# Modulation steps, h^T and scores moved in a two-layer hybrid backbone on one core

## The chip, the core and the metric

The kernel runs on one core of a Trainium2 chip, as one launch. Its time is the device time in microseconds (us), here the median of the runs shown. The engines are TensorE (PE; its weight loads are listed as PEld), VectorE (DVE), ScalarE (ACT), GpSimd (POOL) and SyncE (SP, which only issues DMAs). Each runs its own stream of instructions in order, and they meet at semaphores.

## What is computed

Two layers over 512 latent tokens and, in the first layer and as keys and values in the second, 256 context tokens, all with 1024 channels in float32. Each layer is a sandwich: half a SwiGLU FFN, a token mixer, half a SwiGLU FFN. The mixer is a chunked gMLP in layer 0 and grouped-query attention (8 query heads, 2 key/value heads, RMS-normalised q and k, rotary positions) in layer 1. Cut to what matters here:

```python
m = silu(c) @ w_mod + b_mod                 # 9 vectors of 1024 for each layer and condition
h = x * (1 + scale) + shift                 # modulate
y = (silu(h @ w_g) * (h @ w_u)) @ w_out     # FFN, 1024 -> 2 x 2816 -> 1024
x = layer_norm(ALPHA * x + 0.5 * gate * y, ln_g, ln_b)
# attention: s = q k^T, p = softmax(s), o = p v, then @ w_o; the same kind of closing
```

There are two conditions, one for the latent and one for the context tokens; the last modulation vectors are needed for the latent tokens only.

## The kernel before

Every matrix product is made from float32 values split in two parts of a shorter type: ScalarE casts a high part (`hi`), VectorE subtracts it to make a low part (`lo`), and three matmuls (hi hi, hi lo, lo hi) add up in PSUM. A weight tile comes in by a DMA on SP (`raw`, ring of 6), is split into `w` (ring of 8, `W_BUFS`) and is used some tiles later. `pump(n)` makes up to n splits as far as the ring has room; `release(n)` says that n tiles are used up.

There are six sublayers: FFN, gMLP, FFN (layer 0), FFN, attention, FFN (layer 1). The first, third and fourth are FFNs over 768 tokens in a Strassen form (`tile_strassen`, kind "s"): 22 tiles f, each of seven products (T2, T3, T1, B21 and so on) of 12 matmuls with 384 columns; the first eight tiles (`OPENED`) have two of their products made ahead. Then `out_proj` runs over n = 22 (24 after the gMLP) activation tiles in two halves of the channels: a step x is one weight tile and 18 matmuls, for six blocks of 128 tokens. The last six tiles of the second half (`CLOSE`) are kept for the closing (`End.inner`): block by block the rest of the products, the gated sum (L753, L764), LayerNorm statistics (L765), `rs` (a power on POOL, L184), z normalised on ScalarE (L1911, L1901), then the transposes of the block before (h^T, `h_transposes`) and their modulation (L601, L599) and split (L615, L617). Blocks that are left over are made by `make_h`, called through `self.hooks` from the next sublayer's first projection.

The modulation vectors of later sublayers are made on VectorE as a filler. A step of `mod_unit` multiplies one 128 x 512 tile of w_mod (`mraw`, loaded by SP) into an accumulator, for each of one or two conditions (`light` means one). Eight steps make half a vector; the eighth ends in a `partition_all_reduce` on POOL for each condition and a small DMA on POOL that adds the row to DRAM (L383, L384). `fill` does one step, and counts down `pending` (read-backs of finished vectors); `fill_pair` does two steps if `light`. In the tiles from f = 8 on one `fill_pair` goes with product T3; in `out_proj` most steps x have one. `MOD_PLAN` says which vectors a sublayer makes: 48 steps in the first, 96 in the gMLP, 32 in the third and 64 in the fourth. What is left is done at the closing's beginning.

`out_proj` runs with VectorE and ScalarE pinned, that is in the order of the program; TensorE, SP and most of POOL always are. Elsewhere (attention, the closings) the framework's planner puts their instructions in order by its own costs.

In attention, `token_proj` multiplies blocks of 128 tokens with eight weight tiles. For the second half of q it has three groups of blocks (0 and 1; 2; 3), between which `between` is called. Scores of unit n (a head and a block) go to a pair of PSUM banks, of which there are two (`PAIRS`); VectorE takes the maximum (L1435), ScalarE the exponential (L1443), which frees the pair.

## Time and profile before

| | before |
|---|---|
| median of 3 runs | 2837.98 us (2836.8 to 2839.62) |
| profiled execution, its own time | 2836.91 us |
| its span, first to last instruction | 2835.1 us |
| TensorE busy | 2777.8 us, 98% |
| VectorE busy | 2101.0 us, 74% |
| ScalarE busy | 1164.2 us, 41% |
| POOL busy | 540.4 us, 19% |
| mean granted TensorE clock | 0.996 of full |

Busy times are unions over the span: matmuls overlap in the pipeline, so the mean length of one, times their number, is more than the busy time. [...] A wait is idle time of an engine with the instruction, on which engine, that ended it. The names in a row are those of the tiles: `ps` and `pp` PSUM banks and pairs of banks, `w` split weights, `acc` modulation accumulators, `z` the residual stream.

### The profile page before, as it was taken

The page shows a single profiled execution, that of the slowest core. Times are in us where ns is not written, and L with a number is a line of the kernel's source. Part 1 is how long each engine was busy: PE and PEld are TensorE (multiplying, and loading weights), DVE is VectorE, ACT ScalarE, POOL GpSimd, SP SyncE. Part 2 cuts the span into 40 slices and gives each one's busy share as a digit, 9 for nine tenths or more (in the row PEclk, how much of TensorE's full clock was granted, in tenths as well). Part 3 has the DMA queues.
Part 4 walks back from the last instruction along what each step waited for, and adds up shares of the span by engine and source line. Part 5 has one row for each costly group of instructions (what it writes and reads, how often), then busy time and mean ns, then how long its engine had stood idle before and what let it go on. Part 6 is the DMA issues. An engine that isn't in the chain of part 4 may idle for free.

```text
span 2835.1 us, 40732 instructions
## 1 busy us (share of the span) xinstructions
PE 2777.8 (98%) x14454; PEld 2503.0 (88%) x14454; DVE 2101.0 (74%) x3680; ACT 1164.2 (41%) x2244; POOL 540.4 (19%) x605
## 2 busy tenths in 40 slices
PE   7999999999999999999999999999999999999998
PEld 5999988788899988899999879999988788888886
DVE  6988888577687786698887659888886598634345
ACT  7433332532355532453334236333432666623322
POOL 1000143333321132200013220001233121000001
PEclk9999999999999999999999999999999999999999
DMA  7443376355565474344336534433585424354352
GB/s 230 136 131 117 107 236 212 113 195 189 187 181 161 148 252 136 122 142 136 120 112 209 172 111 133 143 121 119 153 296 175 141 67 88 117 156 130 116 167 86
DMA packets 398675, 429.99 MB, mean 152 GB/s; under 512 B 28488, under 2 KB 287624, under 8 KB 398472
## 3 DMA queue, kind: packets, MB, share of 16 engines
q1 hardware_dynamic: 364360, 319.40, 36.6%
q0 software_dynamic: 34112, 108.00, 12.2%
q8 instruction: 113, 1.85, 0.3%
q14 instruction: 90, 0.74, 0.1%
HBM read 366.10 MB, written 63.41 MB: 151 GB/s over the span
## 4 chain that ended last, share of the span: by engine, by line
PE 86%; DVE 5%; issue 3%; ACT 3%; DMA 2%; POOL 1%; SPq 0%; DVEq 0%; POOLq 0%; ACTq 0%
PE ps L89 85%; PE pp L89 1%; DMA raw<-in_w_mod_dram 1%; ACT z L1911 1%; DVE w L89 1%; POOL acc L383 1%; ACT q L601 1%; DVE comb L89 1%; DMA mraw<-in_w_mod_dram 1%; POOL rs L184 0%; DMA raw<-in_ffn_w_in_dram 0%; DVE w L156 0%; DVE z L89 0%; DVE acc L89 0%; DVE q L1340 0%
## 5 line engine op out<-in xcount | busy, mean ns | idle before, releaser
L89 PE MATMUL ps<-comb,w 128*128 128x384 f32 x5544 | 970.6, 335 | 6.2 <-ACT w L155 2.4
L89 PEld LDWEIGHTS ps<-comb,w 128*128 128x128 f32 x5544 | 961.1, 188 | 11.5 <-ACT w L155 3.0
L89 PE MATMUL ps<-w,acts 128*128 128x512 f32 x3768 | 861.3, 390 | 0.0
L89 PEld LDWEIGHTS ps<-w,acts 128*128 128x128 f32 x3768 | 707.3, 188 | 146.5
L89 ACT CAST w<-raw 128x512 fp32r<-128x512 f32 x630 | 388.3, 620 | 844.4 <-PE ps L89 741.1
L89 DVE TENSOR_TENSOR w<-raw,w 128x512 fp32r<-128x512 f32 x630 | 448.6, 719 | 243.9 <-ACT w L89 243.7
L89 PE MATMUL ps<-h,w 128*128 128x384 f32 (+2 forms) x2304 | 445.6, 353 | 0.2 <-DVE w L156 0.2
L89 PEld LDWEIGHTS ps<-h,w 128*128 128x128 f32 x2304 | 403.0, 188 | 37.7 <-DVE w L156 0.4
L89 DVE SCALAR_TENSOR_TENSOR acc<-mraw,cs,acc 128x512 f32<-128x512 f32 x378 | 278.5, 773 | 15.3 <-DMA mraw<-in_w_mod_dram 15.1
L89 PE MATMUL ps<-w,h 128*128 128x512 f32 x1200 | 276.7, 391 | 2.8 <-ACT h L615 2.8
L89 PEld LDWEIGHTS ps<-w,h 128*128 128x128 f32 x1200 | 225.0, 188 | 50.9 <-ACT h L615 3.6
L383 POOL PARTITION_ALL_REDUCE acc<-acc x56 | 203.4, 3635 | 283.9 <-DVE acc L89 262.3
L89 POOL DMA_DIRECT2D q<-act x226 | 128.7, 611 | 563.5 <-DVE acts L89 296.9
L89 DVE TENSOR_TENSOR q<-q,ps 128x384 f32<-128x384 f32 (+1 forms) x258 | 143.8, 557 | 123.2 <-PE ps L89 102.9
L89 POOL DMA_DIRECT2D act<-stage x84 | 48.3, 575 | 976.9 <-DVE stage L89 930.5
L89 ACT CAST w<-sums 128x512 fp32r<-128x512 f32 x198 | 122.7, 620 | 239.9 <-DVE sums L302 117.6
L89 DVE TENSOR_TENSOR acts<-q,acts 128x384 fp32r<-128x384 f32 (+1 forms) x262 | 150.4, 607 | 9.3 <-ACT acts L89 9.3
L89 ACT CAST acts<-q 128x384 fp32r<-128x384 f32 (+1 forms) x262 | 126.2, 519 | 55.2 <-DVE q L89 36.5
L89 DVE TENSOR_TENSOR w<-sums,w 128x512 fp32r<-128x512 f32 x198 | 135.6, 685 | 1.7 <-ACT w L89 1.7
L156 DVE TENSOR_TENSOR w<-raw,w 128x512 fp32r<-128x512 f32 x114 | 75.4, 687 | 26.6 <-ACT w L155 26.0
L184 POOL TENSOR_TENSOR rs<-ve,mhalf 128x1 f32<-128x1 f32 (+3 forms) x47 | 42.1, 896 | 260.2 <-DVE ve L181 133.9
L155 ACT CAST w<-raw 128x512 fp32r<-128x512 f32 x114 | 67.9, 626 | 55.1 <-PE ps L89 31.8
(206 smaller groups left out, 2173.7 us busy)
## 6 DMA issues: line engine op xcount, KB each, us to landing
raw<-in_ffn_w_in_dram SPq DMA_DIRECT2D x400, 256.0 KB, 3.0
mraw<-in_w_mod_dram SPq DMA_DIRECT2D x256, 256.0 KB, 3.5
raw<-in_ffn_w_out_dram SPq DMA_DIRECT2D x176, 256.0 KB, 3.1
q<-act POOLq DMA_DIRECT2D x216, 192.0 KB, 4.3
act<-stage POOLq DMA_DIRECT2D x74, 384.0 KB, 2.9
raw<-in_gmlp_w_in_dram SPq DMA_DIRECT2D x96, 256.0 KB, 4.3
zhat<-z POOLq DMA_DIRECT2D x26, 512.0 KB, 2.9
raw<-in_gmlp_w_out_dram SPq DMA_DIRECT2D x48, 256.0 KB, 3.0
```

The costliest lines, as they stand in the source:

```text
L89: return self.tc.keep_in_program_order(f(*args, **kwargs))
L155: self.act.copy(hi, src)
L156: self.lows.append((key, lambda: self.dve.tensor_tensor(lo, src, hi.bitcast(F32), ALU.subtract)))
L184: self.last_rstd = self.nc.gpsimd.tensor_tensor(rs, ve, self.mhalf[:, 0:1].to_broadcast([P, n]), ALU.pow).ins
L383: nc.gpsimd.partition_all_reduce(accs[c], accs[c], P, bass_isa.ReduceOp.add)
L601: self.act.activation(h32[:, kk], ps[:, s], AF.Identity, bias=bi, scale=sc)
L1911: k.act.activation(k.z[b], k.z[b], AF.Identity, bias=nb, scale=rs)
```

## The change

- `tile_strassen`: tiles f = 8, 12, 16 and 20 call `fill_pair` a second time, with product B21. In the first FFN's `out_proj` an extra `fill` comes with every eighth step x, not every fourth. The second `fill` of a pair no longer counts down `pending`.
- `token_proj`: where hooks are waiting (the first projections after the first and fourth FFN), a hook is also called between the two halves of the second group; before, hooks came only behind a group.
- Attention: behind the first group of q's second half stand only the transposes of q (`first_turned`); behind the second group come scores 0 and 1, the second key head's transposes and their softmax; score 2 with its softmax comes in the middle of the third group. Weights of the next product are pumped there at k = 0 to 3 only (`ahead`), the others from the loop over units on.
- Attention's closing: for the last block, `pump` is called behind the first half of the channels only; both halves still release.
- The last closing (`last`): for blocks 0 to 2 the product and sum with the LayerNorm's rows follow at once rather than behind the next block's sums. VectorE does the first 512 channels with two fused instructions and no help from ScalarE; ScalarE and POOL do the others. The last block's four instructions are reordered, so that the first half is done and sent before the second.

```diff
@@ -496,12 +496,12 @@
             mods.insert(0, self.vectors_rest())
         self.filler = (s for u in mods for s in u)
 
-    def fill(self, n=1):
+    def fill(self, n=1, count=1):
 
         for _ in range(n):
             with self.behind():
                 for x in self.pending:
-                    x[0] -= 1
+                    x[0] -= count
                 due = [x for x in self.pending if x[0] < 0]
                 self.pending = [x for x in self.pending if x[0] >= 0]
                 for _, f in due:
@@ -512,7 +512,7 @@
 
         self.fill()
         if self.light:
-            self.fill()
+            self.fill(1, 0)
 
     @contextmanager
     def behind(self):
@@ -770,7 +770,7 @@
         for half in range(2):
             self.products(banks[half], b, acts, ws[half * n : half * n + n])
             if after:
-                after()
+                after(half)
         return [lambda half=half: self.add_gated(b, half, banks[half], factor, st) for half in range(2)]
 
     def stats(self, nblocks):
@@ -822,7 +822,7 @@
                     self.fill(int(self.light))
                 elif half or x < n - 1:
                     self.fill_pair()
-                    if prev is None and x % 4 == 3:
+                    if prev is None and x % 8 == 3:
                         self.fill()
         assert not residual
         rest = [acts.of(f) for f in orders[1][n - CLOSE :]]
@@ -985,7 +985,7 @@
         step(b3, "T1", lambda: add(w, w, b3))
         if opened is None:
             g = temp()
-            step(b1, "B21", lambda: act.activation(g, b1, AF.Silu), True)
+            step(b1, "B21", lambda: act.activation(g, b1, AF.Silu), True, int(fills > 1))
         c = temp()
         for _ in self.combining or ():
             pass
@@ -1016,7 +1016,7 @@
         acts = Acts(self, FF, TOK, KEPT, READ_BACK, f"act{l}{i}_")
         for f in range(FF):
             opened = self.begun.pop(min(self.begun)) if self.begun else None
-            self.tile_strassen(lambda: acts.place(f), opened, int(f > 7))
+            self.tile_strassen(lambda: acts.place(f), opened, int(f >= OPENED) * (1 + int(f % 4 == 0)))
             if f == OPENED - 1:
                 self.filler_raw()
         self.out_proj(acts, l, i, 0.5, end, prev, 2 if prev else 12)
@@ -1098,7 +1098,7 @@
         self.out_proj_latent(acts, l, i, 0.5, end, prev)
 
 
-    def token_proj(self, blocks, evacuate, fills=1, between=None):
+    def token_proj(self, blocks, evacuate, fills=1, between=None, inside=None, ahead=KD):
 
         banks = {}
 
@@ -1130,13 +1130,18 @@
                             self.flush()
                         evacuate(b, banks[b])
                 self.flush()
+                if k == KD // 2 - 1 and group is groups[-1] and inside:
+                    inside()
+                if k == KD // 2 - 1 and group is groups[1 % len(groups)] and between is None:
+                    self.hook()
                 if group is groups[-1]:
                     self.release(1)
-                    if k < KD - 1:
+                    if k < min(ahead, KD - 1):
                         self.pump(2)
                     self.fill(fills + int(fills and k == 4))
             self.hook()
-        self.pump(2)
+        if ahead == KD:
+            self.pump(2)
 
     def gmlp(self, l, i, nblocks, end, prev):
         nc, io, dve, act = self.nc, self.io, self.dve, self.act
@@ -1485,15 +1490,12 @@
                 for h in range(4)
             ]
 
-        def first_scores():
+        def first_turned():
             for b in range(2):
                 q_transposed(0, b)
+
+        def first_scores():
             sc = [scores(n) for n in range(PAIRS)]
-            for n in range(PAIRS):
-                state[n] = softmax(*sc[n])
-
-        def next_scores():
-            sc = [scores(n) for n in range(PAIRS, AHEAD)]
             k_transposed(1)
             for x in sc:
                 state[x[0]] = softmax(*x)
@@ -1508,7 +1510,12 @@
         k_transposed(0)
         for b in range(2):
             q_norm(0, b)
-        q_proj(1, between=(first_scores, next_scores))
+
+        def next_scores():
+            for n in range(PAIRS, AHEAD):
+                state[n] = softmax(*scores(n))
+
+        q_proj(1, between=(first_turned, first_scores), inside=next_scores, ahead=KD // 2)
         for b in range(2, NB_LAT):
             q_norm(0, b)
         new_qT(0, 1)
@@ -1572,9 +1579,10 @@
             after = None
             if b == NB_LAT - 1:
 
-                def after():
+                def after(half):
                     self.release(4)
-                    self.pump()
+                    if not half:
+                        self.pump()
 
             return self.close(b, banks, outputs(1), wo, 1.0, st[b], after), st[b]
 
@@ -1920,8 +1928,15 @@
     def last(self, nblocks, close):
 
         k = self.k
-        late = None
         k.dve = Pinned(k.tc, k.nc.vector)
+        first, second = slice(0, 512), slice(512, D)
+
+        def scaled(b, mu, rs, s):
+            z = k.z[b][:, s]
+            k.dve.scalar_tensor_tensor(z, z, mu, self.g[:, s], ALU.subtract, ALU.mult)
+            k.dve.scalar_tensor_tensor(z, z, rs, self.b[:, s], ALU.mult, ALU.add)
+            k.sp.dma_start(k.io["out"][0, b * P : b * P + P, s], z)
+
         for b in range(nblocks):
             adds, st = close(b)
             for add in adds:
@@ -1929,25 +1944,17 @@
             mv = k.sm([2], "mv")
             k.dve.bn_aggr(mv, st)
             rs = k.rstd(mv[:, 1:2], 1, eps=Z_EPS)
-            if late:
-                late()
             if b == nblocks - 1:
-                z, mu = k.z[b], mv[:, 0:1]
-                for s in (slice(0, 512), slice(512, D)):
-                    k.dve.scalar_tensor_tensor(z[:, s], z[:, s], mu, self.g[:, s], ALU.subtract, ALU.mult)
-                for s in (slice(0, 512), slice(512, D)):
-                    k.dve.scalar_tensor_tensor(z[:, s], z[:, s], rs, self.b[:, s], ALU.mult, ALU.add)
-                    k.sp.dma_start(k.io["out"][0, b * P : b * P + P, s], z[:, s])
+                scaled(b, mv[:, 0:1], rs, first)
+                scaled(b, mv[:, 0:1], rs, second)
                 break
             nb = k.norm_bias(mv, rs)
-
-            def late(b=b, rs=rs, nb=nb):
-                for eng, s in ((k.dve, slice(0, 512)), (k.nc.gpsimd, slice(512, D))):
-                    z = k.z[b][:, s]
-                    k.act.activation(z, z, AF.Identity, bias=nb, scale=rs)
-                    eng.tensor_tensor(z, z, self.g[:, s], ALU.mult)
-                    eng.tensor_tensor(z, z, self.b[:, s], ALU.add)
-                    k.sp.dma_start(k.io["out"][0, b * P : b * P + P, s], z)
+            z = k.z[b][:, second]
+            k.act.activation(z, z, AF.Identity, bias=nb, scale=rs)
+            k.pool.tensor_tensor(z, z, self.g[:, second], ALU.mult)
+            k.pool.tensor_tensor(z, z, self.b[:, second], ALU.add)
+            scaled(b, mv[:, 0:1], rs, first)
+            k.sp.dma_start(k.io["out"][0, b * P : b * P + P, second], z)
 
 
 def backbone(tc, io):
```

## Rows read from the trace of the kernel before

**Rows 1.** The page, part 1: busy us, share of the span, instructions.

```profile
PE 2777.8 (98%) x14454; PEld 2503.0 (88%) x14454; DVE 2101.0 (74%) x3680; ACT 1164.2 (41%) x2244; POOL 540.4 (19%) x605
```

**Rows 2.** Windows: busy us per engine (instructions), granted clock, DMA share, GB/s.

```profile
1300.00:1500.00 200.00, 200.00 (x1155) 199.71 (x1154) 169.49 (x288) 76.81 (x139) 16.31 (x18) 1.00 0.38 119
...
2300.00:2350.00 50.00, 46.69 (x304) 42.13 (x302) 45.87 (x107) 40.08 (x79) 5.74 (x5) 0.97 0.24 69
```

**Rows 3.** Waits of TensorE, whole span: total us, times, longest us.

```profile
PE ps L89 <- ACT z L1911: 9.3, 8, 4.9
```

**Rows 4.** Timeline (start us, us, work), POOL and VectorE, end of third sublayer.

```profile
1671.93 3.66 POOL L383 PARTITION_ALL_REDUCE acc<-acc  x1 [12.10 <-DVE acc L89]
...
1680.22 0.80 POOL L384 DMA_DIRECT2D mod<-acc  x1 [0.30 <-POOL acc L383]
...
1683.55 0.15 DVE L181 TENSOR_SCALAR ve<-mv 128x1 f32<-128x1 f32 x1
...
1687.94 0.59 POOL L184 TENSOR_TENSOR rs<-ve,mhalf 128x1 f32<-128x1 f32 x1 [6.92 <-issue]
```

**Rows 5.** Timeline of TensorE, the same place.

```profile
1671.63 13.54 PE L89 MATMUL ps<-w,acts 128*128 128x512 f32 x59
...
1690.05 1.97 PE L89 MATMUL ps<-ident,z 128*128 128x128 f32 x8 [4.88 <-ACT z L1911]
...
1704.20 8.44 PE L89 MATMUL ps<-w,acts 128*128 128x512 f32 x36
```

**Rows 6.** Timeline of TensorE, end of the gMLP sublayer.

```profile
1159.73 16.03 PE L89 MATMUL ps<-w,acts 128*128 128x512 f32 x70
...
1176.51 1.10 PE L89 MATMUL ps<-ident,z 128*128 128x128 f32 x8 [0.75 <-ACT z L1911]
...
1188.38 8.46 PE L89 MATMUL ps<-w,acts 128*128 128x512 f32 x36
```

**Rows 7.** Timeline of VectorE, tiles 14 and 15 of the third sublayer.

```profile
1404.22 0.56 DVE L89 TENSOR_TENSOR stage<-q 128x384 f32<-128x384 f32 x1
...
1416.81 1.41 DVE L89 SCALAR_TENSOR_TENSOR acc<-mraw,cs,acc 128x512 f32<-128x512 f32 x2
...
1418.79 1.94 DVE L89 TENSOR_TENSOR stage<-q 128x384 f32<-128x384 f32 x1
...
1422.38 2.89 DVE L89 TENSOR_TENSOR stage<-q 128x384 f32<-128x384 f32 x1 [0.59 <-ACT q L89]
```

**Rows 8.** Timeline of TensorE, third groups of gMLP's and attention's first projections.

```profile
585.28 6.92 PE L89 MATMUL ps<-w,h 128*128 128x512 f32 x28 [1.17 <-ACT h L615]
...
2249.49 2.63 PE L89 MATMUL ps<-w,h 128*128 128x512 f32 x9 [1.61 <-ACT h L615]
```

**Rows 9.** Timeline of TensorE, start of the attention scores.

```profile
2296.60 0.73 PE L89 MATMUL pp<-kT,qT 128*128 128x512 f32 x2 [0.74 <-ACT qT L149]
...
2298.55 2.64 PE L89 MATMUL pp<-kT,qT 128*128 128x512 f32 x10 [1.22 <-DVE qT L150]
...
2321.02 1.32 PE L89 MATMUL pp<-kT,qT 128*128 128x512 f32 x6 [2.07 <-ACT p L1443]
```

**Rows 10.** Timeline of VectorE, ScalarE and TensorE, end of the attention sublayer.

```profile
2450.21 0.68 DVE L753 SCALAR_TENSOR_TENSOR q<-ps,gate 128x512 f32<-128x512 f32 x1
...
2453.67 1.28 ACT L1911 ACTIVATE z<-z,nb,rs 128x1024 f32<-128x1024 f32 x1
...
2456.79 3.69 DVE L156 TENSOR_TENSOR w<-raw,w 128x512 fp32r<-128x512 f32 x6
...
2460.40 0.68 DVE L753 SCALAR_TENSOR_TENSOR q<-ps,gate 128x512 f32<-128x512 f32 x1
...
2467.38 1.97 PE L89 MATMUL ps<-ident,z 128*128 128x128 f32 x8 [4.08 <-ACT z L1901]
```

**Rows 11.** Timeline of VectorE and POOL after the last matmul.

```profile
2826.84 2.35 DVE L89 TENSOR_TENSOR z<-z,rows 128x512 f32<-128x512 f32 x2
...
2826.96 1.68 POOL L1949 TENSOR_TENSOR z<-z,rows 128x512 f32<-128x512 f32 x1
```

## The prediction

> **What bounds the kernel now.** I read the busy shares first, then TensorE's waits, the busy time in stretches, and last the timeline of each engine where TensorE stands still. TensorE is busy for 98% of the span [rows 1]. Outside it there are 2835.1 - 2777.8 = 57 us, and the change adds and removes no matmul, so those 57 us, with the stretches at the lower clock, are all that there is to win. The reader is to see that they are not spread out: the in-projection of 1300 to 1500 us has no idle TensorE at all [rows 2], while the waits have a few large single pieces, up to 4.9 us behind the normalised z of a stage end (L1911) [rows 3]; the others come below. VectorE is the second limit: 169.49 of 200 us in the in-projection, 45.87 of 50 us where attention starts [rows 2].
>
> **The steps of the modulation.** Counting calls of `fill` in the code: before, the third sublayer (layer 0's second FFN) has 14 in its tiles (f = 8 to 21), 12 in the first half of the out-projection and 7 in the second, for 32 steps. The 32nd, which ends in the last pair of partition reductions on POOL, stands at x = 14 of 16. The trace shows the result: the pair begins at 1671.93, and its last DMA is issued at 1680.22 and takes 0.80; the variance for block 0 was ready at 1683.55 + 0.15 = 1683.70, yet POOL began the power (`rs`) only at 1687.94, 4.2 us later, with nothing named as the cause [rows 4]. TensorE stood 4.88 us and went on at the lower clock: eight transposes took 1.97 us, where those of the gMLP's end took 1.10 [rows 5, 6]. From the end of the out-projection's run to the next long run of 36 matmuls this stage needs 1704.20 - (1671.63 + 13.54) = 19.03 us [rows 5]. The gMLP stage, the same loop over the same blocks, needs 1188.38 - (1159.73 + 16.03) = 12.62 us [rows 6]. After the change the tiles f = 8, 12, 16, 20 hold one step more, 18 in all; the 32nd step moves from x = 14 to x = 10, four slots of 18 matmuls of 16.03/70 = 0.229 us [rows 6], 16.5 us. POOL is then free long before 1683.70. I take the whole difference: **-6.4 us**; the bounds are -6.4 and 0, if POOL's delay has another cause.
>
> What the four steps cost: a step with two conditions is two VectorE instructions, 1.41 us together, and one more pair of reductions comes into the tiles. While POOL reduces, the two `stage<-q` products take 1.94 and 2.89 us instead of 0.56: 3.7 us a pair [rows 7]. A tile has 84 matmuls, 84 x 200/1155 = 14.5 us, and VectorE is busy for 169.49/200 of it, 12.3 us, with one step in it [rows 2]. A tile with two steps and a pair needs 12.3 + 1.4 + 3.7 = 17.4 us: VectorE falls 2.9 us behind and makes up 2.2 us in each later tile. The cover is the ring of eight split weights, 12 matmuls or 2.1 us each: zero on TensorE. Without it, 3 sublayers x (4 x 1.4 + 3.7) = 28 us, the upper bound. POOL's queue: in the second half the loads of `acts` at x = 11 to 13 now stand behind the reductions, which hold POOL from 1671.93 to 1681.02, 9.1 us [rows 4], or to 1687.94 if the unnamed delay belongs to them; the values are first used three slots (12.3 us) after their preparation. Taken as zero, bound 3 us. The steps issue their `mraw` loads on SP earlier as well; the ring of six raw tiles covers them.
>
> [...]
>
> In the first FFN the extra fills in the out-projection are halved, so its count stays 59. In the fourth (layer 1's first FFN) the 64 steps finish four slots earlier, but its end has no POOL wait, so nothing. `fill(1, 0)` leaves more time before a read-back: 0.
>
> **The last block's h^T.** With hooks, `make_h` of the last block now stands between the halves of the second group rather than behind it. TensorE waits 1.17 us at the gMLP's third group and 1.61 us at attention's k/v projection, for casts of just that block [rows 8]. Eight transposes, two PSUM banks and eight affine instructions only move, behind 24 matmuls; z of the block is long normalised. **-2.8 us**, bounds -2.8 and 0.
>
> **Attention's start.** Before, scores follow the transposes of q at once: waits of 0.74 and 1.22 us, then 2.07 us for the exponential that frees a pair of banks [rows 9]. The clock mean is 0.97 over 2300 to 2350 us, so 0.03 x 50 = 1.5 us go at the lower level [rows 2]. Now a block's 24 matmuls lie between transposes and scores, the second head's kT comes behind the scores, and the third score stands within the last block. Available: 0.74 + 1.22 + 2.07 + 1.5 = 5.5 us. Against that, `ahead` moves four weight splits from here into units 1 and 3: four VectorE instructions of 3.69/6 = 0.615 us, 2.5 us [rows 10], and as many casts on ScalarE, in front of the maxima that the scores' banks wait for. VectorE has only 50 - 45.87 = 4.1 us free there. I take 5.5 - 2.5 = **-3.0 us**, bounds -5.5 and +2.5 (all waits return, with the splits on top).
>
> **Attention's end.** The last block's sum (L753) of its second half stood behind six weight splits, 2456.79 to 2460.40, and two more splits stood among its successors; TensorE waited 4.08 us [rows 10]. Now only the first half pumps, so four splits lie ahead: L753 at 2456.79 + 4 x 0.615 = 2459.25. In block 2, from L753 to ScalarE's z took 2453.67 - 2450.21 = 3.46 us; the z instruction itself is 1.28 us. So z is ready at 2459.25 + 3.46 + 1.28 = 2463.99, and the transposes start there, not at 2467.38: 3.4 us, and the transposes lose their 1.97 - 1.10 = 0.9 us of slow clock if the wait is short. The four splits taken away must still run before TensorE's next weights, behind or among these, and SP's loads that wait for their raw tiles run as much later; of 4.3 us I take **-4.0**, bounds -4.3 and 0.
>
> **The tail.** Before, block 2's product and sum with the LayerNorm's rows ran behind the last block's sums: two instructions in 2.35 us, at the same time as POOL's 1.68 us [rows 11]. They now run earlier, under the last block's matmuls. In exchange the second step of the last block's first half waits for `rs` from a POOL that is still working on block 2, and POOL's sums now fall on VectorE's adds. **-1.0 us**, bounds -2.3 and +1.0.
>
> Sum: 6.4 + 2.8 + 3.0 + 4.0 + 1.0 = 17.2 us. The profiled execution itself took 2836.91 us (its span is 2835.1), so 2819.7; the median of the runs is 2837.98, 1.1 higher: **2820.8 us**.
>
> **The rivals.**
> 1. Attention gives nothing back. VectorE is nearly full there, so what TensorE no longer waits for in one place it waits for in the next. For: 45.87 of 50 us. Against: VectorE's own idle time, and the 4.08 us wait is a matter of order, not of load. Both attention terms go: 17.2 - 7.0 = 10.2 us, 2827.8. Chance 0.15.
> 2. POOL's 4.2 us is not from the reductions but from the stage end itself. For: no row names the cause. Against: the gMLP's end, with the reductions earlier, lacks it. 17.2 - 6.4 = 10.8 us, 2827.2. Chance 0.06.
> 3. The pair of reductions that comes into the tiles of three sublayers is not covered: 3 x 3.7 = 11.1 us come back, 2831.9. For: VectorE at 85%. Against: the pair that is in the tiles already, at 1418 to 1425 us [rows 7], stops no matmul (200.00 of 200 us busy) [rows 2]. Chance 0.04. [...]
> 4. Slower: VectorE cannot carry the second step in a tile at all, the place being f = 8, 12, 16, 20 of three FFNs. Price 28 us as above against 17.2 gained: 2848.8. It decides from where more than 17 of the 28 us show as TensorE waits, which is when the weight ring is under two weights deep. The lack of any TensorE wait in tiles speaks against it. Chance 0.05.
> 5. The edits cancel or move nothing (within 0.2%, which is 5.7 us and about what a measurement here can tell from no change): chance 0.05.
>
> The forecast holds the remaining 0.65. Faster takes the forecast, rivals 1 and 2 and half of rival 3: 0.65 + 0.15 + 0.06 + 0.02 = 0.88; same 0.02 + 0.05 = 0.07; slower 0.05. The range runs from the sum of the good ends, 6.4 + 2.8 + 5.5 + 4.3 + 2.3 = 21.3 us or 2816.7, with 2 us for noise and the small waits left out, to rival 1 and 2 with 3 us of uncovered VectorE work: 2814 to 2831.
>
> **What would show it.** Right: in the third sublayer the wait before the first transposes falls to about 0.75 us and the last reduction lies four slots earlier; no wait for L615 in the two third groups; the score waits shrink, with no fall of the clock near 2300 us; L1901's wait under 1 us; the last VectorE instruction 1 us nearer to the last matmul. Wrong: TensorE waits inside tiles 8 to 21, or new waits on `pT`, `nm` or `p` in units 1 to 12.

## The result and the profile after

The changed kernel takes **2823.6 us** (median of 4 runs, 2821.61 to 2825.24) where the one before takes 2838.8 us beside it: ratio 0.9947 [0.993, 0.9964]. A second comparison gave 2822.0 against 2836.5 us, 0.995 [0.9937, 0.9962]. The change takes off 14 to 15 us; 17.2 were predicted. The profiled execution has a span of 2822.1 us.

Part 1 of the page, which answers to [rows 1]:

```profile
PE 2774.6 (98%) x14454; PEld 2501.0 (89%) x14454; DVE 2108.2 (75%) x3680; ACT 1161.7 (41%) x2241; POOL 537.6 (19%) x605
```

TensorE has the same matmuls. Outside its busy time there are now 2822.1 - 2774.6 = 47.5 us, 10 less than before; the other 3 us are shorter busy time, the mean granted clock being 0.997 for 0.996. In the kernel before, the clock stood at its lower level (0.50) in three places between 100 us and the last matmul: during or behind the waits of 4.88 us [rows 5], 0.74 and 1.22 us [rows 9] and 4.08 us [rows 10]. TensorE's windows there (us, busy, matmuls, granted clock, DMA share, GB/s):

```profile
1688.60:1695.20 6.60, 5.15 (x16) 0.50 0.20 79
2299.40:2302.80 3.40, 3.40 (x11) 0.51 0.00 0
2466.80:2470.00 3.20, 2.62 (x13) 0.50 0.86 328
```

The changed kernel has no such place there. TensorE was busy for 11.2 us in these windows, so half of that, some 5.6 us (an estimate), is what the lower clock cost; the gain of 14 to 15 us holds these as well as the idle time. The whole busy time shows only 3 us of it, since the first 100 us of this trace are at a lower mean clock than before (0.96 for 0.98 from 18 to 100 us). The same two windows as in [rows 2]:

```profile
1300.00:1500.00 200.00, 199.53 (x1150) 198.91 (x1150) 172.77 (x287) 74.42 (x136) 23.99 (x23) 1.00 0.39 121
2300.00:2350.00 50.00, 46.17 (x330) 42.12 (x329) 47.81 (x110) 42.95 (x90) 3.98 (x5) 1.00 0.30 77
```

The in-projection has more VectorE and POOL work and a first half microsecond of TensorE idle time. Where attention starts the granted clock stays at 1.00, the matmuls of the 50 us are 330 and no longer 304, and VectorE is fuller still.

TensorE's timeline at the end of the third sublayer (answers to [rows 5]), and POOL's there (answers to [rows 4]):

```profile
1654.80 31.44 PE L89 MATMUL ps<-w,acts 128*128 128x512 f32 x138
1686.99 1.09 PE L89 MATMUL ps<-ident,z 128*128 128x128 f32 x8 [0.75 <-ACT z L1919]
...
1698.87 8.44 PE L89 MATMUL ps<-w,acts 128*128 128x512 f32 x36
```

```profile
1661.22 3.46 POOL L383 PARTITION_ALL_REDUCE acc<-acc  x1
1664.99 0.80 POOL L384 DMA_DIRECT2D mod<-acc  x1 [0.30 <-POOL acc L383]
...
1684.87 0.60 POOL L184 TENSOR_TENSOR rs<-ve,mhalf 128x1 f32<-128x1 f32 x1 [16.87 <-DVE ve L181]
```

The last reductions end 20 us before the power, which now starts as soon as its variance is there; the wait is 0.75 us, the transposes run at the higher clock, and the closing needs 1698.87 - (1654.80 + 31.44) = 12.63 us. Predicted were 12.62.

The price is in the tiles. TensorE, VectorE and POOL in the third sublayer, just behind a tile with two steps:

```profile
1402.09 2.17 PE L89 MATMUL ps<-comb,w 128*128 128x384 f32 x11 [0.47 <-DVE q L89]
```

```profile
1395.20 3.01 DVE L89 TENSOR_TENSOR w<-sums,w 128x512 fp32r<-128x512 f32 x1
1398.13 0.68 DVE L89 TENSOR_TENSOR w<-raw,w 128x512 fp32r<-128x512 f32 x1
```

```profile
1390.69 3.44 POOL L383 PARTITION_ALL_REDUCE acc<-acc  x1 [11.46 <-DVE acc L89]
1394.43 1.00 POOL L384 DMA_DIRECT2D mod<-acc  x1 [0.30 <-POOL acc L383]
1395.21 3.45 POOL L383 PARTITION_ALL_REDUCE acc<-acc  x1
```

A subtraction of VectorE (a split) that takes 0.68 us alone takes 3.01 us beside the reduction; behind it VectorE is late with `q`, and TensorE waits 0.47 us. The fourth sublayer has such a wait of 0.48 us; the kernel before has neither. A wait inside tiles 8 to 21 is what the prediction named as a sign of being wrong; it came, but small.

The hook, in TensorE's timeline at the two third groups (answers to [rows 8]): the transposes of the last block stand behind 24 matmuls, and no wait is left.

```profile
573.67 5.71 PE L89 MATMUL ps<-w,h 128*128 128x512 f32 x24
579.22 1.03 PE L89 MATMUL ps<-ident,z 128*128 128x128 f32 x8
580.00 20.22 PE L89 MATMUL ps<-w,h 128*128 128x512 f32 x88
...
2230.28 5.72 PE L89 MATMUL ps<-w,h 128*128 128x512 f32 x24
2235.84 1.03 PE L89 MATMUL ps<-ident,z 128*128 128x128 f32 x8
2236.63 23.61 PE L89 MATMUL ps<-w,h 128*128 128x512 f32 x103
```

The start of the scores (answers to [rows 9]):

```profile
2293.70 2.25 PE L89 MATMUL pp<-kT,qT 128*128 128x512 f32 x12
...
2299.71 1.32 PE L89 MATMUL pp<-kT,qT 128*128 128x512 f32 x6 [0.38 <-ACT p L1448]
...
2309.80 1.32 PE L89 MATMUL pp<-kT,qT 128*128 128x512 f32 x6 [1.73 <-ACT p L1448]
```

The first twelve scores wait for nothing. The exponential that frees a pair of banks still holds TensorE, for 0.38 and 1.73 us. In the first units come waits that the kernel before doesn't have, 0.37 us for `p` (2315.99), 0.82 us for `qT` (2331.10) and 0.60 us for `nm` (2340.07), while one of 1.57 us for `pT` (2350.33 before) is gone. New waits for `p` and `nm` were the other sign of being wrong; these are small too. Attention's end (answers to [rows 10]), VectorE and then TensorE:

```profile
2447.00 2.49 DVE L156 TENSOR_TENSOR w<-raw,w 128x512 fp32r<-128x512 f32 x4
2449.41 0.68 DVE L753 SCALAR_TENSOR_TENSOR q<-ps,gate 128x512 f32<-128x512 f32 x1
2450.01 0.40 DVE L599 TENSOR_SCALAR q<-ps,modA,modB 128x128 f32<-128x128 f32 x1
2450.33 0.68 DVE L764 TENSOR_TENSOR z<-z,q 128x512 f32<-128x512 f32 x1
2450.93 0.40 DVE L599 TENSOR_SCALAR q<-ps,modA,modB 128x128 f32<-128x128 f32 x1
...
2453.75 0.16 DVE L735 SCALAR_TENSOR_TENSOR nb<-mv,rs 128x1 f32<-128x1 f32 x1 [0.46 <-POOL rs L184]
```

```profile
2447.11 0.48 PE L89 MATMUL ps<-h,w 128*128 128x256 f32 x2
...
2455.24 1.10 PE L89 MATMUL ps<-ident,z 128*128 128x128 f32 x8 [1.73 <-ACT z L1909]
```

Four splits stand ahead of L753, as predicted. But the planner has four of the modulation's affine instructions (L599) among the sums, so the wait is 1.73 us, not under 1. They stood there in the kernel before too, 2463.44 to 2465.52, and its trace could have told. VectorE, the first of them, in the kernel before:

```profile
2463.44 0.40 DVE L599 TENSOR_SCALAR q<-ps,modA,modB 128x128 f32<-128x128 f32 x1
```

Last, VectorE's and POOL's end (answers to [rows 11]):

```profile
2816.54 0.75 DVE L89 SCALAR_TENSOR_TENSOR z<-z,rs,rows 128x512 f32<-128x512 f32 x1
```

```profile
2814.07 0.99 POOL L184 TENSOR_TENSOR rs<-ve,mhalf 128x1 f32<-128x1 f32 x1
```

From the last matmul's end (2810.91) to VectorE's end (2817.29) it is 6.38 us, 7.53 before. From there to the end of the span it is 4.81 us, 3.27 before: POOL's closing drain, a control instruction that the rows don't show, takes 7.27 us in the trace and ends at 2821.3; before it took 4.06 us, and with the new last closing alone, where it starts at the same point as here, 2.45 us.

### The profile page after: what moved, and what is told of

Same layout as the page of the kernel before. It is cut to its first block, busy times and chain, and to the rows that moved or that the text cites. A ratio compares the mean times of both kernels' runs of the same rounds, so it can differ in the third digit from the quotient of the medians.

```text
span 2822.1 us, 40753 instructions
## 1 busy us (share of the span) xinstructions
PE 2774.6 (98%) x14454; PEld 2501.0 (89%) x14454; DVE 2108.2 (75%) x3680; ACT 1161.7 (41%) x2241; POOL 537.6 (19%) x605
## 4 chain that ended last, share of the span: by engine, by line
PE 86%; DVE 6%; ACT 3%; issue 3%; POOL 1%; DMA 1%; SPq 0%; POOLq 0%; DVEq 0%; ACTq 0%
PE ps L89 85%; DVE w L89 1%; PE pp L89 1%; ACT z L1919 1%; DMA raw<-in_w_mod_dram 1%; ACT q L601 1%; POOL acc L383 0%; POOL rs L184 0%; DVE z L89 0%; DVE comb L89 0%; ACT p L1448 0%; DVE nm L1440 0%; ACT w L155 0%; ACT w L89 0%; DVE q L1345 0%
## 5 line engine op out<-in xcount | busy, mean ns | idle before, releaser
L89 DVE TENSOR_TENSOR w<-raw,w 128x512 fp32r<-128x512 f32 x630 | 460.5, 738 | 255.5 <-ACT w L89 255.3
L156 DVE TENSOR_TENSOR w<-raw,w 128x512 fp32r<-128x512 f32 x114 | 75.6, 687 | 28.9 <-ACT w L155 28.5
```

Source lines behind the costliest of these rows:

```text
L89: return self.tc.keep_in_program_order(f(*args, **kwargs))
L156: self.lows.append((key, lambda: self.dve.tensor_tensor(lo, src, hi.bitcast(F32), ALU.subtract)))
```

## The experiments

Eleven kernels and one repeat of the changed one ran, in three comparisons; the kernel before had medians of 2837.05, 2837.68 and 2836.48 us in them. Stretches are measured between fixed points of TensorE's timeline: the first transposes of each closing, those of the first key head, and the first product of the sixth sublayer.

### Each part alone

The kernel before with one part of the change, here cut to its core. A ratio of these five is good to about 2.5 us either way, so they are read with the trace beside them. Times are differences of the medians. **The fills:**

```diff
-                    if prev is None and x % 4 == 3:
+                    if prev is None and x % 8 == 3:
...
-            self.tile_strassen(lambda: acts.place(f), opened, int(f > 7))
+            self.tile_strassen(lambda: acts.place(f), opened, int(f >= OPENED) * (1 + int(f % 4 == 0)))
```

> The modulation steps alone (second fill_pair in tiles 8, 12, 16, 20; every eighth x in the first out-projection; count). Theory: the third sublayer's closing takes 12.6 us from the end of the run to the 36 matmuls, as with the whole change, against 19.03 before; one wait of about 0.5 us comes in the tiles of the third and of the fourth sublayer, behind the reductions; the time is 5.4 us below before, 0.19%. Rival (the delay on POOL belongs to the stage end): the closing stays near 19 us and the time does not fall. Rival (VectorE cannot carry the steps): more than 2 us of waits in tiles.

2834.05 us, 0.999 [0.9981, 0.9998]: -3.0 us, less than half of the term. By the trace the closing falls to 12.6 us as in the changed kernel. From the gMLP's closing to the fourth sublayer's it gains 4.7 us (third sublayer 3.34, fourth 1.33), since the wait of 0.47 us behind the doubled tiles is there too. And the end of the span lies 4.89 us behind VectorE's last instruction: the late drain comes with this part, and takes 1.6 us back.

**The hook:**

```diff
+                if k == KD // 2 - 1 and group is groups[1 % len(groups)] and between is None:
+                    self.hook()
```

> The hook in the second group alone. Theory: both waits for L615 (1.17 and 1.61 us) go and nothing comes in their place: 2.8 us less, 0.1%. Rival: the transposes only move the wait to the second half of the second group, and the time is that of before.

2833.72 us, 0.9986 [0.9977, 0.9995]: -3.3 us by the medians, -4.0 by the ratio. Both waits for L615 are gone; the gMLP sublayer gains 1.8 us and attention's k/v projection 2.6, more than the waits of 1.17 and 1.61 us. Besides, the clock falls to 0.50 just behind the wait of 1.61 us in two of the seven traces without the hook (the fills alone at 2246.6 us, attention's end alone at 2251.3) and in none of the seven with it.

**Attention's start:**

```diff
-        q_proj(1, between=(first_scores, next_scores))
+        q_proj(1, between=(first_turned, first_scores), inside=next_scores, ahead=KD // 2)
```

> The start of attention alone (first_turned, first_scores, next_scores, ahead). Theory: TensorE reaches the third unit's scores 3.7 us earlier, counted from the transposes of kT, and 1.4 us of that are given back before the first output product, since VectorE has four more weight splits in the units: 2.3 us net. No fall of the clock near the scores. Rival (VectorE is full, so all is given back): from the transposes of kT to the first output product the time is that of before, 147.0 us.

2836.51 us, 0.9996 [0.9987, 1.0005]: unclear by the time, where 2.3 us were expected. From the first key head's transposes to the closing's first product the trace has 144.86 us, 147.04 before and 144.73 in the changed kernel. Kernels without this edit lie between 144.95 (the fills alone) and 148.63 (the hook alone) there. What tells them apart is the granted clock; TensorE over the stretch, before, with the fills alone, and in the changed kernel:

```profile
2283.18:2430.22 147.04, 138.90 (x890) 0.99 0.37 88
2280.04:2424.99 144.95, 137.34 (x890) 1.00 0.38 90
2275.71:2420.44 144.73, 137.94 (x891) 1.00 0.38 90
```

Of the seven traces without the edit two have no fall of the clock in the stretch, and need 144.95 and 145.29 us; four have one, and need 146.9 to 147.1; the hook alone has two and needs 148.63. The six traces with the edit and with `ahead` have no fall, and need 144.7 to 145.3. So at the higher clock the edit gains next to nothing: what TensorE no longer waits for at the first scores it waits for in the units. What it takes away is the fall of the clock behind the waits at the first scores or for the exponential, some 2 us where it comes. Why it doesn't come in two of the traces without the edit is open.

**Attention's end:**

```diff
-                    self.pump()
+                    if not half:
+                        self.pump()
```

> The pump of attention's closing alone. Theory: the wait for L1901 falls from 4.1 to 1.7 us and the clock does not fall after it: 3.0 us less in all (2.4 of waiting and 0.6 of clock). The last sum stands behind four splits, and four affine instructions of VectorE come among its successors. Rival: the splits taken away come in front of the sum again, and the wait stays above 3.5 us.

2833.79 us, 0.9986 [0.9977, 0.9995]: -3.3 us by the medians, -4.0 by the ratio. The wait for L1901 is 1.73 us, as expected, and the clock doesn't fall behind it. The sixth sublayer, from its first product to the last matmul, takes 363.8 us where it took 367.4, a little more than the 3.0 expected.

**The tail** (all of the change's `last`):

```diff
-            def late(b=b, rs=rs, nb=nb):
...
+            z = k.z[b][:, second]
+            k.act.activation(z, z, AF.Identity, bias=nb, scale=rs)
+            k.pool.tensor_tensor(z, z, self.g[:, second], ALU.mult)
+            k.pool.tensor_tensor(z, z, self.b[:, second], ALU.add)
+            scaled(b, mv[:, 0:1], rs, first)
```

> The last closing alone. Theory: from the last matmul to VectorE's last instruction 6.4 us instead of 7.5, and the span's end 3.3 us after that, as before the change: 1.1 us less in all, since POOL's drain at the end is late only where POOL's stream is longer. Rival (the late drain, 4.8 us from VectorE's last instruction to the end, belongs to the new last closing): nothing or less than 0.3 us is won.

2836.33 us, 0.9995 [0.9986, 1.0004]. From the last matmul to VectorE's end 6.40 us, 7.53 before, and 3.24 us from there to the end: -1.1 us by the trace, and nothing comes back when the fills are not there. The time alone can't tell it from none.

The five ratios leave 0.1 + 0.14 + 0.04 + 0.14 + 0.05 = 0.47%, 13.3 us (the medians 11.5); the whole has 0.50 to 0.53%. The parts add up within what they can be told apart.

### One step in one tile

Is POOL's 4.2 us [rows 4] really due to the last reductions, and how many steps does it take?

```diff
-            self.tile_strassen(lambda: acts.place(f), opened, int(f > 7))
+            self.tile_strassen(lambda: acts.place(f), opened, int(f > 7) + int((f, l, i) == (8, 0, 6)))
```

(With the second `fill_pair` at B21, as in the change; nothing else of it.)

> One extra step, in tile 8 of the third sublayer only. Theory (POOL needs some 6.9 us from a reduction's last DMA to its first instruction of another kind, wherever that falls): the pair begins one slot, 4.1 us, earlier, POOL begins the power at the moment that the variance is ready or at most 0.3 us later, the wait before the first transposes falls from 4.9 to under 1.1 us, and the closing takes 12.6 to 13 us: one step does what four do. Rival (the delay belongs to the stage end): the closing stays at 19 us. Rival (each of the four steps takes a quarter): 17.4 us.

2830.94 us, 0.9979 [0.9969, 0.9989]: -6.7 us by the medians, -6.0 by the ratio and by the trace (from the gMLP's closing to the fourth sublayer's), where the four steps in every sublayer gave 4.7 by the trace and took 1.6 back at the end. POOL:

```profile
1672.39 3.46 POOL L383 PARTITION_ALL_REDUCE acc<-acc  x1
1676.14 0.80 POOL L384 DMA_DIRECT2D mod<-acc  x1 [0.30 <-POOL acc L383]
1684.22 0.59 POOL L184 TENSOR_TENSOR rs<-ve,mhalf 128x1 f32<-128x1 f32 x1 [7.27 <-DVE ve L181]
```

The variance is ready at 1683.70 in this kernel as it was before. The pair's last DMA is issued 4.08 us earlier, and the power starts 3.72 us earlier, 7.28 us behind that issue; before it was 6.92. With the variance ready in both, POOL's start follows the reductions and not the stage end: rival 2 falls. It is still POOL that comes late here, 0.52 us behind the variance; in the changed kernel, with the reductions long over, the power comes 0.09 us behind it. TensorE waits 1.16 us instead of 0.75, and the closing takes 13.03 us, a little over what was expected (1.1 and 13).

### A longer stream on POOL

The kernel before with eight more copies of a small memset at its start, which makes POOL's stream as long as in the changed kernel:

```diff
-        nc.gpsimd.memset(one, 1.0)
+        for _ in range(9):
+            nc.gpsimd.memset(one, 1.0)
```

> Before, with eight more instructions on POOL at the very start (eight repeats of a memset of one column). Theory (the late end belongs to the length of POOL's stream): the last drain of POOL ends 6 us or more after its last power instead of 1.4, and the end of the span lies 4.8 us after VectorE's last instruction instead of 3.3: 1.5 us more. Rival (it belongs to the moved modulation steps): the end is that of before, 3.3 us.

2837.38 us, 0.9999 [0.9989, 1.0008], and the end 3.27 us behind VectorE's. The length alone does not make the drain late, so the theory is wrong. The same edit on the changed kernel:

> The changed kernel with eight more small memsets on GpSimd at the very start, which shift that engine's stream of instructions by eight and do nothing else. If the late end (4.8 us after VectorE's last instruction, 3.3 before) comes from where GpSimd's stream happens to be cut, it moves back to about 3.3; if it comes from the order of the work, it stays at 4.8 and the time is that of the changed kernel within 0.5 us.

2821.36 us, 0.9948 [0.9933, 0.9963], and the end 4.81 us behind VectorE's: it is not the place in the stream either.

### The changed kernel without `ahead`

```diff
-        q_proj(1, between=(first_turned, first_scores), inside=next_scores, ahead=KD // 2)
+        q_proj(1, between=(first_turned, first_scores), inside=next_scores)
```

> The change with the pumps of q's second half as before (ahead left out). Theory (four splits more in the units are what gives back 1.4 us): the units' waits shrink, but eight splits stand in the third group, in front of the first maxima, so the third unit's scores come 2 us later than with the change, counted from the transposes of kT; to the first output product the time lies between the change's 144.7 us and 147.0 of before. Rival (where the splits stand is without effect): 144.7 us, within 0.3.

2825.7 us, 0.996 [0.9945, 0.9974]. The stretch of attention takes 148.97 us, 4.2 more than with `ahead` and 1.9 more than before the change, outside what either theory or rival had. VectorE's timeline shows why:

```profile
2305.26 2.49 DVE L156 TENSOR_TENSOR w<-raw,w 128x512 fp32r<-128x512 f32 x4
2307.67 0.95 DVE L1440 TENSOR_REDUCE nm<-pp 128x1 f32<-128x768 f32 x1
2308.54 0.68 DVE L156 TENSOR_TENSOR w<-raw,w 128x512 fp32r<-128x512 f32 x1
2309.14 1.28 DVE L150 TENSOR_TENSOR qT<-ps,qT 128x512 fp32r<-128x512 f32 x2
```

Four splits and one more stand ahead of the copies of q^T that TensorE waits for, and TensorE waits for them and then for the exponential; from 2312 to 2315 us its granted clock is 0.50, and six score matmuls take 2.29 us for 1.32:

```profile
2309.97 1.01 PE L89 MATMUL ps<-ident,p 128*128 128x128 f32 x6 [1.37 <-DVE qT L150]
2312.26 2.29 PE L89 MATMUL pp<-kT,qT 128*128 128x512 f32 x6 [1.28 <-ACT p L1448]
```

With `ahead` the same copies start at 2305.51. So `ahead` is no cost of 2.5 us. Of the 4.2 us some 2 are longer waits, and the rest is put down to the fall of the clock behind them (an estimate). The size is from one trace, of the slowest of four runs (2828.47 us; the others 2825.03 to 2826.3). By the ratios, 0.996 beside 0.9947 and 0.995, `ahead` earns about 3 us, and the intervals overlap.

### The changed kernel again, and two attempts to better it

Beside the two attempts ran the changed kernel itself:

> The changed kernel itself, beside the other three of this comparison: about 2823.6 us, 0.995 of the time before, with the end of the span again 4.8 us after VectorE's last instruction if that lateness belongs to this kernel, 3.3 if it came by chance in the one profile seen so far.

2822.02 us, 0.995 [0.9937, 0.9962]; the end 4.80 us behind VectorE's again.

The first attempt doubles other tiles and fixes VectorE's order in the last block of attention's closing:

```diff
-... int(f >= OPENED) * (1 + int(f % 4 == 0)))
+... int(f >= OPENED) * (1 + int(f in (8, 11, 15, 20))))
...
+            if b == nblocks - 1 and nblocks == NB_LAT:
+                k.dve = Pinned(k.tc, k.nc.vector)
```

> The changed kernel with two of its four double tiles moved to others of a sublayer (8, 11, 15, 20 in place of 8, 12, 16, 20), and VectorE's order in the last block of attention's closing kept as written. Theory: the waits of 0.47 and 0.48 us that follow a double tile sit where they do by the tile's place among the reductions, and so go (about -1 us), and TensorE's wait of 1.73 us at attention's end falls below 0.7 once no other work stands among the block's sums (about -1.1); sum about 2 us under the changed kernel. Rival: the waits come back at other tiles, and the first opening part then waits for splits that the pinned order has pushed behind the sums; the time stays within 1 us of the changed kernel.

2824.28 us, 0.9958 [0.9946, 0.9971]. The waits of 0.47 and 0.48 us are gone, but the way is hardly shorter: from the first closing to the sixth sublayer it takes 1906.4 us (the changed kernel 1906.6 and 1907.5, before 1918.6). But the fixed order loses 2.85 us in the sixth sublayer (366.65 us). VectorE and TensorE there:

```profile
2446.11 0.68 DVE L89 SCALAR_TENSOR_TENSOR q<-ps,gate 128x512 f32<-128x512 f32 x1
...
2449.12 0.68 DVE L89 TENSOR_TENSOR h<-q,h 128x512 fp32r<-128x512 f32 x1
```

```profile
2449.85 5.95 PE L89 MATMUL ps<-h,w 128*128 128x256 f32 x35 [3.46 <-DVE h L89]
2455.64 1.04 PE L89 MATMUL ps<-ident,z 128*128 128x128 f32 x8
```

Behind the sums and splits now stands the split of h that the running product needs. TensorE waits 3.46 us for it, before the transposes, which then wait for nothing, and the clock falls to 0.50 behind the wait (2450.0 to 2453.4 us). The planner's order with its 1.73 us is the better one. The second half of the rival is what happened, and the time is 2.3 us above the changed kernel's.

The second attempt leaves out the fills' part and gives two steps more to the third sublayer alone, with the same fixed order:

```diff
-... int(f >= OPENED) * (1 + int(f % 4 == 0)))
+... int(f > 7) + int((l, i) == (0, 6) and f in (8, 10)))
```

> The changed kernel with extra modulation steps in two tiles of the third sublayer alone (8 and 10) instead of four in each, and the same fixed order at attention's end. Theory (the four doubled tiles buy no more than the step or two that the third sublayer's end needs, and cost 0.5 us a sublayer): closing of the third sublayer 12.6 us from its last pass to the next large product as in the changed kernel, no in-tile waits beyond those of the kernel before, the fourth sublayer gives up nothing: 1 to 2 us under the changed kernel, 1.5 more if the late end goes too. Rival (all four steps needed): the third closing goes back to 13 us or more, and the time is that of the changed kernel or above.

2822.07 us, 0.995 [0.9938, 0.9963]. The wait at the third sublayer's end is 0.75 us, the tiles have only the waits of the kernel before, the way to the sixth sublayer takes 1905.6 us, and the end is 3.24 us behind VectorE's. The sixth sublayer loses the same 2.86 us to the fixed order, so the kernel is no faster than the changed one, where 1 to 2 us were expected. Without that order it should take about 2822.1 - 2.9 = 2819 us; this is an estimate, and was not run.

## Why the prediction was right, by its steps

The time came out 2.8 us above the forecast in the first comparison and 1.2 in the second, in the range and on the side that had most of the chance. No rival happened as a whole: attention gave 6 us by the trace (rival 1; but its reason holds for the start of attention, see below), POOL's delay went with the reductions (rival 2), the uncovered part of the reductions is a wait of half a microsecond in two sublayers and not 3.7 in three (rival 3), and VectorE carries the second step (rival 4). That the sum came so near is in part luck: the fills gave 3.3 us less than their term and the last block's h^T 1.6 more, and neither was foreseen.

| term | predicted | by the trace | the part alone, medians (ratio) |
|---|---|---|---|
| fills | -6.4 | closing -6.4; with the tiles -4.7; with the end -3.1 | -3.0 (-2.8) |
| h^T of the last block | -2.8 | -1.8 and -2.6 | -3.3 (-4.0) |
| attention's start | -3.0 | -2.3, a fall of the clock | -0.5 (-1.1) |
| attention's end | -4.0 | -3.6 | -3.3 (-4.0) |
| tail | -1.0 | -1.1 | -1.4 (-1.4) |

**Fills.** The place and the size of the closing's gain were right to 0.01 us. The mis-sized term is the cover, "zero on TensorE". The ring of weights does cover VectorE's lag; `q` of the running tile, which has no ring, is what comes late. The two waits seen make 0.95 of the 1.7 us between -6.4 and -4.7; the rest was not placed. The need for four steps a sublayer was never questioned: one, in one sublayer, gave all but 0.4 us of the closing, and two gave all of it.

**h^T.** Under-sized: the term was made from the two largest waits, and the stages gained about 1.6 us more (1.8 + 2.6 against 2.8). Other traces bear it out: the gMLP sublayer takes 637.7 to 638.2 us in the seven without the hook and 636.0 to 636.4 in the seven with it; the k/v projection takes 80.7 to 81.1 us in the five without it that have no fall of the clock there, and 78.1 to 78.6 with it. So half a microsecond or more at each place comes on top of the wait's idle time; where it comes from was not traced. The fall of the clock to 0.50 behind the wait of 1.61 us, in two of the seven traces without the hook, was not in the term at all.

**Attention's start.** The sum was near and its parts were not. Available were 5.5 us, of which 0.38 + 1.73 us for the exponential stayed. The waits of 0.74 and 1.22 us went, but others in the units took their place, as rival 1 argued; what was won is the term's 1.5 us for the clock and a little more. The 2.5 us put down for `ahead` had the wrong sign: the splits it moves were in the way of q^T and the maxima where they stood, and it earns some 3 to 4 us. The error was to price the splits only where they arrive, and at nothing where they leave.

**Attention's end.** L753 comes 2.30 us behind the first product, where 2.35 was predicted. From L753 to z it took 4.53 us in place of the 3.46 taken from block 2, because of the four L599 among the sums; that is the whole miss at this wait. The last block's own rows in the kernel before had them, and were the ones to take.

**Tail.** Right at -1.1 by the trace. The end of the program was not in the sum at all: POOL's drain, 1.5 us later because of the fills, takes more than that back.

## What to carry to other kernels

When a wait goes with one moved step, move that one step before giving the same to every tile: here one step in one tile was worth 6.7 us alone, and twelve doubled tiles 3.0. A wait can cost more than its idle time (in the kernel before, the granted clock was 0.50 from 1688.6 to 1695.2 us, with the wait of 4.88 us): look at the granted clock behind it, and compare traces of several kernels at that place before a gain is put down to an edit. Price moved work at both its ends, since leaving a crowded place can be worth more than arriving at another costs. A chain measured in one block holds for the next only as long as the planner keeps other work out of it; and fixing the order by hand needs a look at all who wait on that engine, not only the last.

## What the hardware showed

In these traces POOL takes about 7 us to go from its reductions to the power, and as long for the way back. The power behind reductions starts 6.92 us after their last DMA is issued, with no releaser named ("issue") [rows 4]. POOL's timeline in the kernel before, a power in the gMLP sublayer and a reduction behind the attention sublayer, each with the row ahead of it:

```profile
756.94 3.95 POOL L1179 DMA_DIRECT2D v_spill<-q  x6 [9.92 <-ACT q L89]
767.87 1.37 POOL L184 TENSOR_TENSOR rs<-ve,mhalf 128x6 f32<-128x6 f32 x1 [6.98 <-issue]
...
2564.27 0.54 POOL L89 DMA_DIRECT2D act<-stage  x1 [10.34 <-DVE stage L89]
2572.55 3.25 POOL L383 PARTITION_ALL_REDUCE acc<-acc  x1 [7.74 <-issue]
```

The fourteen traces hold 154 changes between the two kinds (DMA issues between left out), none with less than 6.3 us of idle POOL directly in front; in the 34 that have no other releaser it is 6.6 to 8.0 us. Instructions of one kind have no such gap where they wait for nothing: in the kernel before, a power comes 0.08 us behind a sum (2816.19 us), and the second reduction of the pair at 1676.47 us has no idle POOL ahead of it. The page of the profile shows this as an unnamed delay, which the prediction could only bound by its absence elsewhere; where POOL stood idle for longer before the power of a stage end (10.59, 10.93 and 21.06 us in the kernel before, 10.93, 16.87 and 24.36 us in the changed one), it is hidden, and the power comes 0.09 or 0.10 us behind its variance. What takes this time was not found; in the delay of [rows 4], 1681.0 to 1687.9 us, the trace has no transfer on an instruction queue, and no DMA at all in the last 5 us.

Open is the late drain of POOL. It came in every kernel with doubled tiles in all three sublayers (the fills alone 4.89 us behind VectorE's end, the changed kernel 4.80 to 4.81, also with the shifted stream and without `ahead`; 4.75 with the other four tiles) and in none without them (3.24 to 3.28). The same kernels have the halved extra fills of the first FFN, which were not tried by themselves. It is neither the length of POOL's stream nor the place of its start; what in the fills brings it was not found. One trace of it is left: the six traces with the late drain, and none of the eight others, have one more 8 KB transfer on an instruction queue (q14) behind the end of the span, at 2823.8 us in the changed kernel. It comes after the drain, so it is not its cause.
